# Gate layout with operands made another way, and 19 instead of 14 early first-layer products

## The chip, the cores and the metric

One core of a Trainium2 chip runs the whole program. The metric is the device time of one execution, in microseconds. Engines are named as in the profile: PE (matrix products; PEld is its weight load), DVE (vector), ACT (activation), POOL (GpSimd), SP (which here only issues DMAs).

## The reference, cut to what matters

One layer works on 1024 tokens of width 1024: a token mixer (gated linear attention and windowed attention), a layer norm, then a channel mixer that retrieves experts, and a last layer norm. The change lies in the channel mixer. For each token and each of 8 heads it takes the 16 best of 16384 experts by product keys (two lists of 128 keys); an expert has the number 128 * i1 + i2, a row u and a row v:

```
gate = jax.nn.softmax(top_s, axis=-1)
u = peer_u[eidx]
v = peer_v[eidx]
act = jax.nn.gelu(jnp.einsum('pd,phkd->phk', xt, u))
y = jnp.einsum('phk,phkd->pd', gate * act, v)
```

## The kernel before, in words

The kernel handles the channel mixer in two ways. For the first ND = 5 of 8 token tiles (640 tokens) it is **dense**: all 16384 experts are computed, as 128 expert tiles (jj) of 128 experts. A *product* (products(), L880 and below) is the first layer of one expert tile: the rows u are loaded in two pieces, split into a high part on ACT (uhi, L888) and a low part (ulo, L889), and two halves of 320 tokens are each summed from 8 x 3 matmuls (mm3, L115 to L117) into PSUM. Gelu, multiplication by the gates of that tile (L1059) and a split into high and low parts (L110, L111) give the weights W; outputs() then does the second layer for a pair of expert tiles (60 matmuls into pyd, added to yacc, L1087). For the last NS = 3 tiles (384 tokens) it is **sparse**: each step gathers the rows u, v of one expert for each of 128 tokens (L965) and uses DVE, ACT and POOL (L982, L998, L999).

**The gate layout** (gates(), L783 to L824) writes, for the 5 dense tiles, the gates as a dense array g_d of experts by tokens. It works on GG = 4 tokens at a time, 32 groups for each token tile, 160 in all. For each token, a matrix of 128 selected experts by 128 one-hot columns of i2 (oa) and one of i1 times the gate (ob), both in f32, are multiplied on PE (8 matmul instructions for a group, L819), and ACT copies the result out of PSUM (gstage, L821). Before, DVE makes both one-hots as wa and wb, bf16, with the four tokens innermost (L808, one instruction each); ACT copies wa into oa, with the tokens outermost (L809, one instruction); ob comes from wb in four ACT copies with the gate as scale (L815), in every fourth group instead in one DVE multiplication (L811). wa and wb share six buffers; oa and ob have four each.

**The order.** weave() (L95) takes generators, each with a number of steps and a span, and calls next() on them in the order of evenly spaced times. When it has used up all steps it runs each generator to its end, in the order in which they were given. After the token mixer one weave issues four: the gate layout (made, 152 steps), the retrieval for the last pair of token tiles (after = picks(3), 34 steps, span 0 to 0.7), the early products (early(), two steps for each) and the first 20 sparse steps. The retrieval of that pair has yielded once ahead of the weave (next(after), L869); it still has the 8 yields of best() and 13 in each of two calls of retrieval() (1 after the sums, 4 over the heads, 8 over the product sums, L733 to L740). What follows the last yield, such as chosen[j] at L760, runs when next() is called again. The order of issue is a priority only: a list scheduler puts each engine's instructions in an order of its own by estimated times, and each engine then runs in that order.

**Early products.** For the expert tiles in EARLY (0 to 3, then 12, 24, ... 120: 14) the product and its gelu are done in that weave, on the gate stage's PE, with the low part on POOL, and stored in act_d (L1014 to L1020). The loop of the dense stage (L1108 and below) loads them (gearly, L1054) and goes straight to the gates. The sparse steps are spread over the dense stage by progress (advance()).

In the profiled execution the token mixer takes the time up to about 860 us, the gate stage lasts from there to 1345, the dense stage from 1345 to the end.

Of the kernel before, what the change touches and what calls it, by code (L numbers as in the profile page):

```python
# [10 lines left out]
F32 = mybir.dt.float32  # L11
F32R = mybir.dt.float32r
BF = mybir.dt.bfloat16
I32 = mybir.dt.int32
U32 = mybir.dt.uint32
AF = mybir.ActivationFunctionType
OP = mybir.AluOpType
# [20 lines left out]
def kernel(ctx: ExitStack, tc: tile.TileContext, A, out):  # L38
    nc = tc.nc
    V, S, G, PE = nc.vector, nc.scalar, nc.gpsimd, nc.tensor  # L40

    def pool(stack, name, bufs=1, side="left", space=None):
        kw = {"space": space} if space == bass.MemoryType.DRAM else {"side": side, "reuse_waits": "tile"}
        if space == bass.MemoryType.PSUM:
            kw["space"] = space
        return stack.enter_context(tc.tile_pool(name=name, bufs=bufs, **kw))
# [6 lines left out]
    def acc(name):  # L53
        return ps.tile([128, 512], F32, tag="acc", name=name, bufs=4)
# [11 lines left out]
    iota = cst.tile([128, 128], F32, name="iota")  # L66
# [21 lines left out]
    g_d = drm.tile([TD // GT, 128, 128, GT], F32, name="g_d")  # L88
    act_d = [drm.tile([128, TD], F32, name=f"act_d{j}") for j in range(len(EARLY))]

# [4 lines left out]
    def weave(*parts):  # L95

        parts = [(g, n, *(at or (0, 1))) for g, n, *at in parts]
        order = sorted((a + (s + 0.5) / n * (b - a), i) for i, (_, n, a, b) in enumerate(parts) for s in range(n))
        for _, i in order:
            next(parts[i][0], None)  # L100
        for g, *_ in parts:
            for _ in g:
                pass
# [22 lines left out]
    with ExitStack() as px:  # L126
# [39 lines left out]
        early = px.enter_context(ExitStack())  # L166
# [278 lines left out]
    with ExitStack() as mx:  # L445
        xp = pool(mx, "xp", side="right")
        wb = pool(mx, "wb", side="right")
# [6 lines left out]
        def affine():  # L454
            pin(nc.scalar.dma_start(l1g, A["ln1_g"].to_broadcast([128, D])))
            pin(nc.scalar.dma_start(l1b, A["ln1_b"].to_broadcast([128, D])))
            pin(nc.scalar.dma_start(subk, A["subk"]))
            row = tk.tile([128, NCAND], F32, tag="c2", name="row", bufs=1)
            pin(nc.scalar.dma_start(row, A["iotac"].to_broadcast([128, NCAND])))
            V.tensor_copy(iotac, row[:, :, None].to_broadcast([128, NCAND, 8]))  # L460
            for i in range(2):
                nc.sync.dma_start(cols[:, i, :], mod_d[2 - i].rearrange("(k p) -> p k", p=128))
            V.tensor_scalar(cols[:, 0], cols[:, 0], 1.0, None, OP.add)
            yield
# [300 lines left out]
        def picks(pair, hh2):  # L765
            tv = tk.tile([128, 2, 2, NH, TOPK], F32, name="tv")
            ti = tk.tile([128, 2, 2, NH, TOPK], U32, name="ti")
            sc = []
            if pair == ORDER[-1]:
                for _ in scores(hh2, sc):  # L770
                    pass
            else:
                for a, b in zip(scores(hh2, sc), best(sc, tv, ti)):
                    yield
            yield
            if pair == ORDER[-1]:
                yield from best(sc, tv, ti)
            for i in range(2):
                yield from retrieval(2 * pair + i, tv[:, i], ti[:, i])

        gb, todo = [], []

        def gates():  # L783

            while not gb:
                yield
            wide = gb[0].tile([128, 128, GG], BF, name="wide", bufs=1)
            V.tensor_copy(wide, iota[:, :, None].to_broadcast([128, 128, GG]))
            for _ in range(ND):
                while not todo:  # L790
                    yield
                j = todo.pop(0)
                ej = gb[0].tile([128, 128], I32, name="ej", bufs=1)
                nc.sync.dma_start(ej, e_d[j])
                gj = gb[0].tile([128, 128], F32, name="gj", bufs=1)
                nc.sync.dma_start(gj, gt_d[j])
                i12 = gb[0].tile([128, 2, 128], I32, name="i12", bufs=1)
                V.tensor_scalar(i12[:, 0], ej, 127, None, OP.bitwise_and)
                V.tensor_scalar(i12[:, 1], ej, 7, None, OP.logical_shift_right)
                f12 = gb[0].tile([128, 2, 128], BF, name="f12", bufs=2)  # L800
                V.tensor_copy(f12, i12)
                for q in range(0, 128, GG):
                    if q % GT == 0:
                        gs = gb[0].tile([128, 128, GT], F32, name="gstage", bufs=2)
                    w = [gb[0].tile([128, 128, GG], BF, tag="wab", name=n, bufs=24 // GG) for n in ("wa", "wb")]
                    o = [gb[0].tile([128, GG, 128], F32, name=n, bufs=16 // GG) for n in ("oa", "ob")]
                    for i in range(2):
                        V.tensor_tensor(w[i], wide, f12[:, i, None, q:q + GG].to_broadcast([128, 128, GG]), OP.is_equal)  # L808
                    S.activation(o[0], w[0].rearrange("p i t -> p t i"), AF.Copy)  # L809
                    if SCALE[q // GG % len(SCALE)]:  # L810
                        V.tensor_tensor(o[1], w[1].rearrange("p i t -> p t i"),  # L811
                                        gj[:, q:q + GG, None].to_broadcast([128, GG, 128]), OP.mult)
                    else:
                        for c in range(GG):
                            S.activation(o[1][:, c], w[1][:, :, c], AF.Copy, scale=gj[:, q + c:q + c + 1])  # L815
                    for h in range(0, GG, 4):
                        p = acc("pgb")
                        for c in range(4):
                            PE.matmul(p[:, c::4], o[0][:, h + c], o[1][:, h + c], start=True, stop=True)  # L819
                        t = q % GT + h  # L820
                        S.activation(gs[:, :, t:t + 4], p.rearrange("p (j t) -> p j t", t=4), AF.Copy)  # L821
                    if q % GT == GT - GG:
                        nc.scalar.dma_start(g_d[128 // GT * j + q // GT], gs)
                    yield  # L824

        def pairs():
# [4 lines left out]
            while tiles or front or back or groups:  # L831
# [4 lines left out]
                for m in front + back:  # L836
                    m[1] += 1
                    try:
# [9 lines left out]
                        else:  # L848
                            back.remove(m)
                            if m[2] % 2:  # L850
                                yield m[2] // 2, hh2s[m[2] // 2]

        after, made = affine(), gates()
        turn = beat = 0.0
        for ready in pairs():
# [9 lines left out]
            if ready:  # L865
                for _ in after:
                    pass
                after = picks(*ready)
# [142 lines left out]
    with ExitStack() as gx:  # L1011
        ue = pool(gx, "ue", side="right")

        def early():  # L1014
            for i, jj in enumerate(EARLY):
                for h, p in products(jj, ue, ps, (3, 2, 2), G):
                    ga = ue.tile([128, HW], F32, name="gact", bufs=2)
                    S.activation(ga, p, AF.Gelu)
                    nc.sync.dma_start(act_d[i][:, HW * h:HW * h + HW], ga)
                    yield  # L1020

        steps = sparse_steps()

        def first():

            for _ in range(FIRST):
                next(steps)
                done[0] += 1
                yield

        done = [0]
        weave((made, GLEFT, *SPANS[0]), (after, 34, *SPANS[1]), (early(), 2 * len(EARLY), *SPANS[2]), (first(), FIRST, *SPANS[3]))
    px.close()
    front.close()

# [7 lines left out]
    def gated(jj, h):  # L1043
# [7 lines left out]
        w = wts[jj]  # L1051
        if jj in EARLY:
            ga = ep.tile([128, HW], F32, name="gearly", bufs=2)
            nc.sync.dma_start(ga, act_d[EARLY.index(jj)][:, HW * h:HW * h + HW])  # L1054
        else:
# [36 lines left out]
    yacc = ep.tile([128, ND, D], F32, name="yacc")  # L1092
    filled = [jj for jj in range(128) if jj not in EARLY][:FILL]
    for jj in filled:
# [36 lines left out]
WB = 7  # L1131
PICK = 1.3
GATE = 1
SCALE = (0, 0, 0, 1)
GLEFT = 152
SPANS = ((0, 1), (0, 0.7), (0.5, 1), (0.2, 0.8))
EARLY = [0, 1, 2, 3] + list(range(12, 128, 12))
UB = 3
BATCH = 2
FIRST = 20  # L1140
# [5 lines left out]
GG = 4  # L1146
# [118 lines left out]
```

## Time and profile before

| | us |
|---|---|
| median of 3 runs | 3193.69 |
| lowest, highest | 3190.36, 3199.3 |
| the profiled execution, its own time | 3201.31 |
| span of its profile | 3199.5 |

The span runs from the first to the last instruction; 1.8 us of the time lie around it. In a windows view each line gives a stretch, its length, the busy time of each engine (instructions counted as busy are joined where they overlap) with the number of instructions in brackets, the clock granted to PE as a share of full speed, the share of the DMA engines' time in use, and GB/s. In a groups view the number ahead of the bar is the count, behind it the busy time and the mean duration of one, then the idle time in front of such instructions and what ended it. Durations on one engine overlap a little, so the sum of busy times of groups can exceed the stretch.

### The profile page before, as it was taken

How to read it: one execution, taken by the hardware profiler on the slowest of the kernel's cores; microseconds unless marked ns; L12 is line 12 of the kernel's file. 1: busy time of each engine (PE TensorE's matmuls, PEld its weight loads, DVE VectorE, ACT ScalarE, POOL GpSimd, SP SyncE). 2: the span in 40 equal slices, each digit the busy share in tenths (PEclk: the TensorE clock that was granted, in tenths of full speed). 3: DMA queues.
4: the chain of work that ended last, by engine and by line, in shares of the span. 5: the costliest groups of instructions: out<-in, count | busy, mean ns of one | idle time of the engine just before them, and what ended most of it. 6: DMA issues, size and time to landing. Idle time of an engine off the chain costs nothing. (4 is left out here: it accounts for less than half of the span.)

```text
span 3199.5 us, 48912 instructions
## 1 busy us (share of the span) xinstructions
PE 2840.5 (89%) x16604; PEld 2456.4 (77%) x16604; DVE 2561.7 (80%) x5718; ACT 1614.6 (50%) x3437; POOL 1669.0 (52%) x1111
## 2 busy tenths in 40 slices
PE   6998878879777788789999999999999999999893
PEld 3677756757567787678889888888888888888782
DVE  4318834578788997469988988999988999999898
ACT  3324534342547889834555444555444545445452
POOL 0012301052543551026777776778768777778676
PEclk9999989889888899999999999999999999999996
DMA  9653655646465567577889898989889998989884
GB/s 331 218 188 112 215 213 198 213 171 207 148 219 186 227 217 265 221 235 284 321 323 327 314 328 305 321 322 336 328 310 326 331 328 304 323 307 330 295 292 171
DMA packets 352679, 848.82 MB, mean 265 GB/s; under 512 B 27627, under 2 KB 165611, under 8 KB 299692
## 3 DMA queue, kind: packets, MB, share of 16 engines
q1 hardware_dynamic: 285520, 384.20, 36.7%
q0 software_dynamic: 55296, 402.68, 33.0%
q10 hardware_dynamic: 11612, 58.81, 4.7%
q8 instruction: 131, 2.15, 0.3%
q14 instruction: 120, 0.98, 0.1%
HBM read 745.43 MB, written 100.16 MB: 264 GB/s over the span
## 5 line engine op out<-in xcount | busy, mean ns | idle before, releaser
L999 POOL TENSOR_TENSOR ys<-ys,uv 128x1024 f32<-128x1024 f32 x362 | 900.9, 2489 | 407.7 <-ACT uv L998 374.8
L117 PE MATMUL pact<-hhD,ulo 128*128 128x320 f32 x2048 | 633.4, 316 | 57.0 <-DVE ulo L889 36.7
L115 PE MATMUL pact<-hhD,uhi 128*128 128x320 f32 x2048 | 641.2, 314 | 5.8 <-ACT uhi L888 2.9
L116 PE MATMUL pact<-hhD,uhi 128*128 128x320 f32 x2048 | 638.0, 313 | 0.0
L115 PE MATMUL pyd<-vhi,W 128*128 128x512 f32 x1280 | 516.0, 403 | 39.8 <-DVE yacc L1087 32.9
L965 POOL DMA_INDIRECT uv<-in_uv_dram,ex x384 | 408.4, 1064 | 249.4 <-DVE ys L996 75.5
L116 PE MATMUL pyd<-vlo,W 128*128 128x512 f32 x1280 | 504.4, 394 | 0.0
L117 PE MATMUL pyd<-vhi,W 128*128 128x512 f32 x1280 | 502.6, 396 | 0.0
L998 ACT ACTIVATE uv<-uv,w 128x1024 f32<-128x1024 f32 x362 | 396.6, 1144 | 171.2 <-DVE w L987 105.2
L982 DVE SCALAR_TENSOR_TENSOR uv<-uv,h2p 128x1024 f32<-128x1024 f32 x384 | 462.8, 1208 | 11.6 <-DMA uv<-in_uv_dram,ex 7.5
L1087 DVE TENSOR_TENSOR yacc<-yacc,pyd 128x512 f32<-128x512 f32 x630 | 417.4, 676 | 45.3 <-PE pyd L117 43.2
L117 PEld LDWEIGHTS pact<-hhD,ulo 128*128 128x128 f32 x2048 | 388.9, 191 | 78.4 <-DVE ulo L889 47.0
L115 PEld LDWEIGHTS pact<-hhD,uhi 128*128 128x128 f32 x2048 | 392.7, 192 | 21.1 <-ACT uhi L888 4.5
L116 PEld LDWEIGHTS pact<-hhD,uhi 128*128 128x128 f32 x2048 | 392.1, 191 | 10.7
L115 PEld LDWEIGHTS pyd<-vhi,W 128*128 128x128 f32 x1280 | 243.0, 190 | 89.0 <-DVE yacc L1087 39.9
L889 DVE TENSOR_TENSOR ulo<-uraw,uhi 128x512 fp32r<-128x512 f32 x228 | 266.1, 1173 | 30.1 <-ACT uhi L888 28.2
L111 DVE TENSOR_TENSOR vlo<-vraw,vhi 128x512 fp32r<-128x512 f32 x256 | 279.3, 1112 | 10.4 <-ACT vhi L110 10.1
L117 PEld LDWEIGHTS pyd<-vhi,W 128*128 128x128 f32 x1280 | 242.2, 190 | 57.9
L116 PEld LDWEIGHTS pyd<-vlo,W 128*128 128x128 f32 x1280 | 243.6, 190 | 39.0
L819 PE MATMUL pgb<-ob,oa 128*128 128x128 f32 x1280 | 200.8, 306 | 54.7 <-ACT ob L815 42.5
L819 PEld LDWEIGHTS pgb<-ob,oa 128*128 128x128 f32 x1280 | 182.5, 208 | 69.7 <-ACT ob L815 53.1
L110 ACT ACTIVATE W<-pact 128x320 fp32r<-128x320 f32 x222 | 95.5, 431 | 240.8 <-DVE pact L1059 234.6
(357 smaller groups left out, 5234.1 us busy)
## 6 DMA issues: line engine op xcount, KB each, us to landing
uraw<-in_ut_dram SPq DMA_DIRECT2D x256, 256.0 KB
vraw<-in_uv_dram SPq DMA_DIRECT2D x256, 256.0 KB
g_d<-gstage ACTq DMA_DIRECT2D x20, 2048.0 KB
gload<-g_d SPq DMA_DIRECT2D x32, 1280.0 KB
wo<-wo_d SPq DMA_DIRECT2D x64, 512.0 KB
wq<-wq_d SPq DMA_DIRECT2D x64, 512.0 KB
wt<-in_w_ada_dram SPq DMA_DIRECT2D x48, 512.0 KB
wq_d<-wqs SPq DMA_DIRECT2D x16, 512.0 KB
```

Source lines behind the costliest of these rows:

```text
L110: S.activation(hi, src, AF.Copy)
L111: eng.tensor_tensor(lo, src, hi.bitcast(F32), OP.subtract)
L115: PE.matmul(out_, l[0], r[0], start=(k == 0), stop=False)
L116: PE.matmul(out_, l[0], r[1], start=False, stop=False)
L117: PE.matmul(out_, l[1], r[0], start=False, stop=(k == n - 1))
L819: PE.matmul(p[:, c::4], o[0][:, h + c], o[1][:, h + c], start=True, stop=True)
L889: lower.tensor_tensor(lo, raw, hi.bitcast(F32), OP.subtract)
L965: G.indirect_dma_start(out=uv[n][0].rearrange("p a d -> p (a d)"), out_offset=None, in_=A["uv"], in_offset=bass.IndirectOffsetOnAxis(ap=ch ...
L982: pin(V.scalar_tensor_tensor(t[:, 0], t[:, 0], 1.0, h2[j], OP.mult, OP.mult, accum_out=w[:, i:i + 1]))
L998: S.activation(v, v, AF.Copy, scale=wb)
L999: G.tensor_tensor(ys[j], ys[j], v, OP.add)
L1087: V.tensor_tensor(ya, ya, p, OP.add)
```

## The change

The gate layout gets a second flag list, `retrieved`, and two branches. Without the flag, DVE writes oa itself, as f32 (comparing a plain row of numbers with each token's i2), makes wb as before, and all four scaled copies into ob are ACT's, in every group. With the flag, wa goes through ACT as before, and ob comes from four DVE instructions on 128 x 128, each a comparison and a multiplication by the gate. The flag is set by rest(), a generator that runs the retrieval of the last pair to its end and then appends to the list; it takes the place of `after` in the weave, with the same 34 steps. A bf16 copy of the row (once) and an f32 copy of i1 (f2, once for each token tile) are added. SCALE is gone. The span of the retrieval goes from 0.7 to 0.6 and that of the early products begins at 0.35 instead of 0.5. EARLY becomes 0 to 3 and 8, 16, ... 120: 19 expert tiles.

```
--- before.py
+++ after.py
@@ -778,7 +778,7 @@
             for i in range(2):
                 yield from retrieval(2 * pair + i, tv[:, i], ti[:, i])
 
-        gb, todo = [], []
+        gb, todo, retrieved = [], [], []
 
         def gates():
 
@@ -786,6 +786,8 @@
                 yield
             wide = gb[0].tile([128, 128, GG], BF, name="wide", bufs=1)
             V.tensor_copy(wide, iota[:, :, None].to_broadcast([128, 128, GG]))
+            row = gb[0].tile([128, 128], BF, name="iotab", bufs=1)
+            V.tensor_copy(row, iota)
             for _ in range(ND):
                 while not todo:
                     yield
@@ -799,20 +801,31 @@
                 V.tensor_scalar(i12[:, 1], ej, 7, None, OP.logical_shift_right)
                 f12 = gb[0].tile([128, 2, 128], BF, name="f12", bufs=2)
                 V.tensor_copy(f12, i12)
+                f2 = gb[0].tile([128, 128], F32, name="f2", bufs=2)
+                V.tensor_copy(f2, i12[:, 1])
+
+                def wide_hot(i, q):
+
+                    w = gb[0].tile([128, 128, GG], BF, tag="wab", name=("wa", "wb")[i], bufs=24 // GG)
+                    V.tensor_tensor(w, wide, f12[:, i, None, q:q + GG].to_broadcast([128, 128, GG]), OP.is_equal)
+                    return w
+
                 for q in range(0, 128, GG):
                     if q % GT == 0:
                         gs = gb[0].tile([128, 128, GT], F32, name="gstage", bufs=2)
-                    w = [gb[0].tile([128, 128, GG], BF, tag="wab", name=n, bufs=24 // GG) for n in ("wa", "wb")]
                     o = [gb[0].tile([128, GG, 128], F32, name=n, bufs=16 // GG) for n in ("oa", "ob")]
-                    for i in range(2):
-                        V.tensor_tensor(w[i], wide, f12[:, i, None, q:q + GG].to_broadcast([128, 128, GG]), OP.is_equal)
-                    S.activation(o[0], w[0].rearrange("p i t -> p t i"), AF.Copy)
-                    if SCALE[q // GG % len(SCALE)]:
-                        V.tensor_tensor(o[1], w[1].rearrange("p i t -> p t i"),
-                                        gj[:, q:q + GG, None].to_broadcast([128, GG, 128]), OP.mult)
+                    if retrieved:
+                        w = wide_hot(0, q)
+                        S.activation(o[0], w.rearrange("p i t -> p t i"), AF.Copy)
+                        for c in range(GG):
+                            V.tensor_scalar(o[1][:, c], iota, f2[:, q + c:q + c + 1], gj[:, q + c:q + c + 1],
+                                            OP.is_equal, OP.mult)
                     else:
+                        V.tensor_tensor(o[0], row[:, None, :].to_broadcast([128, GG, 128]),
+                                        f12[:, 0, q:q + GG, None].to_broadcast([128, GG, 128]), OP.is_equal)
+                        w = wide_hot(1, q)
                         for c in range(GG):
-                            S.activation(o[1][:, c], w[1][:, :, c], AF.Copy, scale=gj[:, q + c:q + c + 1])
+                            S.activation(o[1][:, c], w[:, :, c], AF.Copy, scale=gj[:, q + c:q + c + 1])
                     for h in range(0, GG, 4):
                         p = acc("pgb")
                         for c in range(4):
@@ -1029,7 +1042,12 @@
                 yield
 
         done = [0]
-        weave((made, GLEFT, *SPANS[0]), (after, 34, *SPANS[1]), (early(), 2 * len(EARLY), *SPANS[2]), (first(), FIRST, *SPANS[3]))
+        def rest():
+
+            yield from after
+            retrieved.append(True)
+
+        weave((made, GLEFT, *SPANS[0]), (rest(), 34, *SPANS[1]), (early(), 2 * len(EARLY), *SPANS[2]), (first(), FIRST, *SPANS[3]))
     px.close()
     front.close()
 
@@ -1131,10 +1149,9 @@
 WB = 7
 PICK = 1.3
 GATE = 1
-SCALE = (0, 0, 0, 1)
 GLEFT = 152
-SPANS = ((0, 1), (0, 0.7), (0.5, 1), (0.2, 0.8))
-EARLY = [0, 1, 2, 3] + list(range(12, 128, 12))
+SPANS = ((0, 1), (0, 0.6), (0.35, 1), (0.2, 0.8))
+EARLY = [0, 1, 2, 3] + list(range(8, 128, 8))
 UB = 3
 BATCH = 2
 FIRST = 20
```

## Rows read from the trace of the kernel before

**Rows 1.** The page: busy shares, then PE over 40 equal slices.

```profile
PE 2840.5 (89%) x16604; PEld 2456.4 (77%) x16604; DVE 2561.7 (80%) x5718; ACT 1614.6 (50%) x3437; POOL 1669.0 (52%) x1111
PE   6998878879777788789999999999999999999893
```

**Rows 2.** Windows of the gate stage: columns as named in its first line.

```profile
core 0: us, PE busy (x) PEld busy (x) DVE busy (x) ACT busy (x) POOL busy (x), PEclk, DMA share, GB/s
1100.00:1183.00 83.00, 66.51 (x453) 65.27 (x452) 80.64 (x175) 64.25 (x159) 45.31 (x41) 0.89 0.57 208
1183.00:1226.00 43.00, 42.96 (x325) 42.77 (x324) 33.04 (x64) 41.44 (x109) 14.61 (x12) 1.00 0.77 289
1226.00:1345.00 119.00, 87.32 (x506) 75.95 (x504) 71.27 (x155) 118.58 (x311) 7.88 (x9) 0.93 0.56 214
860.00:1345.00 485.00, 383.23 (x2544) 355.84 (x2544) 396.52 (x1405) 380.62 (x964) 169.21 (x177) 0.90 0.62 221
```

**Rows 3.** Two lines of the kernel: last product sums and early gelus, first and last start.

```profile
L740 DVE TENSOR_REDUCE ee<-oh x64: 388/833/1734, 674.7 to 1180.0; 128x16 f32<-128x160 f32 x24, 128x16 f32<-128x400 f32 x24, 128x16 f32<-128x320 f32 x8, 128x16 f32<-128x800 f32 x8
...
L1018 ACT ACTIVATE gact<-pact x28: 409/418/469, 1020.0 to 1225.3; 128x320 f32<-128x320 f32 x28
```

**Rows 4.** Groups by line, 1226 to 1345: xcount | busy us, mean ns | idle, releaser.

```profile
L815 ACT ACTIVATE ob<-wb,gj 128x128 f32<-128x128 bf16 x180 | 60.3, 415 | 0.0
L809 ACT ACTIVATE oa<-wa 128x512 f32<-128x512 bf16 x60 | 40.2, 674 | 0.0
L821 ACT ACTIVATE gstage<-pgb 128x512 f32<-128x512 f32 x64 | 37.6, 599 | 0.5 <-PE pgb L819 0.5
L808 DVE TENSOR_TENSOR wa<-wide,f 128x512 bf16<-128x512 bf16 x57 | 24.1, 422 | 21.6 <-ACT ob L815 13.1 <-ACT oa L809 7.5 <-ACT gstage L821 0.8
L811 DVE TENSOR_TENSOR ob<-wb,gj 128x512 f32<-128x512 bf16 x15 | 10.4, 691 | 1.4
```

**Rows 5.** Groups by line, 1100 to 1183: the operands on DVE.

```profile
L808 DVE TENSOR_TENSOR wa<-wide,f 128x512 bf16<-128x512 bf16 x28 | 16.8, 599 | 0.0
L811 DVE TENSOR_TENSOR ob<-wb,gj 128x512 f32<-128x512 bf16 x7 | 6.2, 888 | 0.1
```

**Rows 6.** Groups by line, 855 to 1345: the ACT parts of a product.

```profile
L888 ACT ACTIVATE uhi<-uraw 128x512 fp32r<-128x512 f32 x28 | 17.2, 624 | 2.6 <-issue 1.8 <-POOL ce L709 0.8
L1018 ACT ACTIVATE gact<-pact 128x320 f32<-128x320 f32 x28 | 11.8, 424 | 0.9 <-PE pact L117 0.8
```

**Rows 7.** Groups by line, 1183 to 1226: one gstage copy for each group.

```profile
L821 ACT ACTIVATE gstage<-pgb 128x512 f32<-128x512 f32 x17 | 9.9, 581 | 0.8 <-PE pgb L819 0.8
```

**Rows 8.** Windows 1698.6 to 3050.8: eight stretches of six pairs, one and sum.

```profile
2038.00:2201.20 163.20, 161.28 (x890) 144.81 (x889) 151.37 (x243) 85.62 (x146) 130.08 (x72) 1.00 0.92 331
...
sum 1352.20, PE 1305.54 PEld 1165.83 DVE 1239.30 ACT 675.30 POOL 1003.49; mean PE 163.19 PEld 145.73 DVE 154.91 ACT 84.41 POOL 125.44
```

**Rows 9.** Windows of two pairs: with one product, with two.

```profile
2038.00:2058.90 20.90, 20.90 (x110) 18.29 (x109) 18.50 (x28) 11.48 (x18) 17.56 (x10) 1.00 0.89 326
2058.90:2086.90 28.00, 28.00 (x158) 25.34 (x157) 25.48 (x44) 14.81 (x26) 24.44 (x14) 1.00 0.99 357
```

**Rows 10.** Windows of the eight pairs ahead of those of rows 11: sum.

```profile
sum 250.50, PE 233.02 PEld 208.82 DVE 227.42 ACT 119.16 POOL 183.50; mean PE 29.13 PEld 26.10 DVE 28.43 ACT 14.89 POOL 22.94
```

**Rows 11.** Windows of the eight pairs that begin those stretches (early tile): sum.

```profile
sum 173.40, PE 173.40 PEld 152.35 DVE 160.33 ACT 87.53 POOL 124.67; mean PE 21.68 PEld 19.04 DVE 20.04 ACT 10.94 POOL 15.58
```

**Rows 12.** Groups by line, 1500 to 2900: products and gating on DVE.

```profile
L889 DVE TENSOR_TENSOR ulo<-uraw,uhi 128x512 fp32r<-128x512 f32 x182 | 212.3, 1173 | 10.4 <-ACT uhi L888 8.8 <-ACT uv L998 0.7 <-issue 0.2
L1059 DVE TENSOR_TENSOR pact<-pact,gload 128x320 f32<-128x320 f32 x182 | 89.0, 489 | 31.6 <-ACT pact L1057 29.5 <-ACT uv L998 1.6 <-issue 0.3
L111 DVE TENSOR_TENSOR W<-pact,W 128x320 fp32r<-128x320 f32 x182 | 87.4, 481 | 16.1 <-ACT W L110 11.5 <-ACT uv L998 4.4
L111 DVE TENSOR_TENSOR W<-gearly,W 128x320 fp32r<-128x320 f32 x18 | 24.3, 1368 | 0.5 <-ACT W L110 0.5
L1059 DVE TENSOR_TENSOR gearly<-gearly,gload 128x320 f32<-128x320 f32 x16 | 10.8, 715 | 4.3 <-DMA gload<-g_d 4.1
```

## The prediction

> **What bounds the kernel now.** The page comes first: PE is busy for 89% of the span, and its slices read 7 and 8 up to about the fifteenth and 9 from the twentieth on [rows 1]. So there are two regimes, a gate stage in which PE has room and a dense stage in which it has hardly any. The change moves five products from the second to the first.
>
> The windows show what bounds the gate stage [rows 2]. From 1100 to 1183, while the last retrieval runs (its last sums start at 1180, [rows 3]), DVE is busy for 80.6 of 83 us. From 1183 to 1226 both ACT (41.4) and PE (43.0) fill the 43 us, with the last products in them (the last gelu starts at 1225, [rows 3]). From 1226 to 1345 only gate groups and a few sparse steps are left, ACT is busy for 118.6 of 119 us and PE for 87.3. So DVE bounds until 1183, ACT after that. Of the 160 groups, each with one gstage copy, 17 + 64 = 81 come after 1183 [rows 4, 7] and 79 before.
>
> In the dense stage a pair of expert tiles is the unit, counted from its first matmul into pyd to the next pair's. A pair with two products takes 28.0 us with PE busy for all of them, one with a single product (the other tile is early) 20.9 [rows 9]. A product is therefore worth **7.1 us** where PE bounds. Eight stretches of six pairs, one of the six early in each, take 1352.2 us, 169.0 each [rows 8], against 5 x 28.0 + 20.9 = 160.9 with PE full: 8.1 us are lost elsewhere. DVE is busy for 1239 of the 1352 us, so it stands close behind PE.
>
> **First, what the change does.** The second way of making the operands is never used. rest() has 34 steps in the weave, and the retrieval has 34 yields left: 8 from best(), 13 from each of two tiles. The 34th step stops at the last yield. The flag is set behind it, at a 35th call, and that comes only when weave() runs its generators out; the gate layout stands first there and has used up its 160 groups by then. So all 160 groups take the branch without the flag: oa from DVE in f32, all of ob on ACT, no 128x128 DVE comparisons.
>
> **Gate stage, DVE.** A group loses wa and a fourth of an ob multiplication and gains one f32 comparison of 128x512. No row shows that comparison. Below, it costs what wa does (599 ns while POOL works, 422 later), above, what L811 does, 888 and 691 ns [rows 4, 5]. I take the upper end: L811 has the same shape, f32 output and one operand spread over the innermost axis. Each of the 79 groups before 1183 costs 888 - 599 - 7/28 x 888 = 67 ns more: **+5 us** on the engine that bounds there; at the lower end 222 ns less, -18. The f2 and row copies are six small instructions, under 599 ns each: +1, at most 4. wb stays, and neither removed instruction has anyone else waiting on it.
> VectorE: DVE Perf Modes in the Trainium skill (section "Mode 2×_1P — pack two bf16 into one 32-bit read") says that two results a cycle need every tensor to be 16-bit. That speaks against the change: the f32 output would take the slow rate, which is the upper end; if the fast rate held, the sum would be 23 us lower.
>
> **Gate stage, ACT.** In the last window ACT's groups add up to 138 us in 118.6 busy ones [rows 2, 4], so instructions overlap and each counts 0.85 of its duration. A group loses oa (0.85 x 674 = 573 ns) and gains a fourth of four ob copies (353 ns): -220 ns; -18 us for the 81 groups after 1183. An added product brings two uhi and two gelus, 0.85 x 2 x (624 + 424) ns [rows 6] = 1.8 us: +9 for five. Net **-9 us** where ACT bounds.
>
> **Gate stage, PE.** The five products bring 5 x 7.1 = 36 us. PE idles for 102 of 485 us there, 32 of them after 1226 [rows 2]. If all five come after 1226, PE needs 87.3 + 36 = 123 us for what took 119: +4. If some find room before, as the earlier span allows, ACT sets the end: -9. I take about 0 (-9 to +4), nearer PE's end, since PE was full whenever products ran after 1183. The low parts are POOL's, which is busy for 7.9 us after 1226. The ten added loads from SP's queue and ten stores of gelus fall where DMA is at 0.56 to 0.77. SP waits for nothing new. The earlier retrieval span shifts DVE work ahead of gate groups without adding any; nothing. Gate stage: +5 + 1 + 0 = **+6 us**, the end moving from 1345 to 1351.
>
> **Dense stage.** Five tiles lose their products, so early pairs come every fourth instead of every sixth. With PE full, the 60 pairs from expert tile 8 on take 15 x (3 x 28.0 + 20.9) = 1574 instead of 10 x 160.9 = 1609: **-36 us**. What becomes of the other loss, 8.1 us in six pairs, decides the rest. The pair ahead of an early one takes 250.5 / 8 = 31.3 us [rows 10], the early one 173.4 / 8 = 21.7 [rows 11], the other 32 of the 48 take (1352.2 - 250.5 - 173.4) / 32 = 29.0 [rows 8]. An early tile thus saves 29.0 - 21.7 = 7.3 and costs its forerunner 2.3: 5.0 each, **-25 us** for five. The ends: if the loss is spread by time, 36 x 169.0 / 160.9 = -37; if it all hangs on early tiles, 15 x 8.1 - 10 x 8.1 = 40 us come back, +5. I keep the measured split.
> DVE gains nothing from an early tile: it saves two ulo (1173 ns each), but both halves of its gating read SBUF instead of PSUM, 715 against 489 and 1368 against 481 ns [rows 12], which is 2.2 us given back of 2.3. SBUF — State Buffer in the Trainium skill (section "SBUF: two separate sides") says that a DVE instruction with two SBUF inputs and a GpSimd one that reads SBUF exclude each other for a whole instruction; the 1368 agrees. The sparse steps are spread over 117 units of progress instead of 119.5, so they keep their pace in time, and DMA at about 0.9 stays there: the rows u of five tiles go, the stored gelus come.
>
> **Sum.** +6 - 25 = **-19 us**. The profiled execution took 3201.3 us (span 3199.5 and 1.8 around it), 7.6 above the median 3193.7; I apply the difference to the median: **3175 us**. A change under 0.3%, 9.6 us, can hardly be told from none; faster means under 3184, slower over 3203.
>
> **Rivals.**
> The dense stage gives its full PE share (-37) and ACT sets the end of the gate stage without DVE being later (-9): 3194 - 46 = 3148; a comparison at wa's price takes off 18 more at the utmost. For it: pairs run at exactly 28.0 at a time. Against it: DVE close behind PE. Chance 0.15, faster.
> DVE takes PE's place: early tiles carry most or all of the loss, the dense stage comes out between -6 and +5, and with the gate stage's +6 the time is 3194 to 3205. For it: DVE at 1239 of 1352 us with its work unchanged. Against it: the measured 2.3 is not 8.1. Chance 0.2, mostly no change.
> Slower: PE's fixed order puts the five products between the last gate groups, and ACT waits at gstage behind them. Then the 36 us come on top of the last stretch, whose 32 us of PE idle time stay: +36 + 6 - 25 = +17, **3211 us**. It decides if the idle time after 1226 is not filled by more than 8 us. For it: between 1183 and 1226 PE is already full. Against it: three buffers of raw rows and POOL at 7.9 of 119 us let products run ahead. Chance 0.13.
> The flag does come in time: ACT's part of a late group falls to oa and gstage, 0.85 x (674 + 599) = 1.1 us, PE's +4 sets the end after 1226, 3175 to 3179. Chance 0.02; it would show in DVE instructions of 128x128 in gates().
>
> **How the numbers follow.** The forecast has 0.5. Faster: 0.45 of it (its own range is 3160 to 3187), 0.15 of the first rival and the flag's 0.02: 0.62. No change: 0.05 of the forecast and 0.18 of the second rival: 0.23. Slower: the third rival and 0.02 of the second: 0.15. The range goes from 3148, the first rival without its utmost, to 3203, the second rival's end; it leaves out the slow case and a few hundredths below.
>
> **What would show it.** After the change there must be 160 DVE comparisons into oa of 128x512 f32 near 690 to 890 ns, 640 ACT copies into ob, none into oa. The gate stage should end within 8 us of 1351, with ACT below 119 of its last 119 us and PE above 100. In the dense stage 15 pairs of about 21 us, forerunners near 31. I am wrong if the comparison takes 420 ns, if the gate stage ends over 15 us off, or if the pairs without an early neighbour grow beyond 29.5, with DVE as what PE waits for.

## The result, and the profile after

The kernel after takes **3232.15 us** (median of 4 runs, 3226.78 to 3236.67), that before 3196.49 beside it; the ratio is 1.0114, interval 1.0095 to 1.0132. It is slower by some 36 us, where 3175 was forecast. The profiled execution has a span of 3228.4 us, 28.9 more than before.

The page of the kernel after, as in [rows 1]:

```profile
PE 2840.1 (88%) x16604; PEld 2456.1 (76%) x16604; DVE 2638.9 (82%) x5674; ACT 1573.1 (49%) x3437; POOL 1689.9 (52%) x1121
PE   6998878978778889898999899999999999999980
```

DVE is busy for 77 us more, PE for as long as before. Windows show where. First the kernel before: the gate stage stands in [rows 2]; here are the 63 pairs, from the first matmul into pyd to that of the last pair, and the rest.

```profile
1370.70:3131.40 1760.70, 1690.20 (x9110) 1504.83 (x9109) 1598.95 (x2520) 868.36 (x1497) 1274.48 (x718) 0.99 0.87 313
3131.40:3199.50 68.10, 17.15 (x62) 12.49 (x60) 56.01 (x70) 18.75 (x26) 41.60 (x20) 0.63 0.42 162
```

The kernel after: the gate stage, the 63 pairs, the rest (columns as in [rows 2]).

```profile
860.00:1326.00 466.00, 392.90 (x2771) 373.73 (x2770) 423.38 (x1355) 345.16 (x968) 188.57 (x187) 0.94 0.66 236
1351.60:3121.60 1770.00, 1675.92 (x8870) 1483.28 (x8869) 1621.12 (x2482) 843.47 (x1459) 1237.11 (x696) 0.97 0.85 304
3121.60:3228.40 106.80, 17.77 (x62) 12.87 (x60) 79.55 (x98) 32.68 (x43) 79.65 (x42) 0.59 0.54 211
```

The first pair starts at 1351.6 instead of 1370.7, **19 us earlier**. The pairs take **9 us longer**, with 240 matmuls less. From the last pair's start to the end it takes **39 us longer**. -19 + 9 + 39 = 29, the whole difference.

Of these 19 us, 7 lie ahead of the change. The token mixer, the same code in both kernels, ends with this instruction on DVE (eight of them, duration min/median/max in ns, first and last start); the last one starts at 852.9 before and at 845.9 after:

```profile
L111 DVE TENSOR_TENSOR mT<-ao,mT x8: 661/678/693, 458.8 to 852.9; 128x512 fp32r<-128x512 f32 x8
L111 DVE TENSOR_TENSOR mT<-ao,mT x8: 667/678/692, 454.5 to 845.9; 128x512 fp32r<-128x512 f32 x8
```

From there to the end of the last gstage copy (1344.8 and 1325.9) the gate stage takes 492 us before and 480 after: it is **12 us shorter**. The change costs 36 us by the traces, then, as it does by the medians.

**The gate stage.** Groups by line, 860 to 1326, of the kernel after:

```profile
L828 ACT ACTIVATE ob<-wb,gj 128x128 f32<-128x128 bf16 x624 | 205.0, 411 | 3.5 <-DMA gj<-gt_d 2.9 <-DVE wb L810 0.6
L824 DVE TENSOR_TENSOR oa<-iotab,f 128x512 f32<-128x512 bf16 x156 | 125.2, 809 | 15.9 <-PE pgb L832 15.4
L834 ACT ACTIVATE gstage<-pgb 128x512 f32<-128x512 f32 x160 | 94.1, 595 | 31.9 <-PE pgb L832 24.9 <-DMA hhD<-hh_d 6.5 <-ACT ob L828 0.2
```

There are no 128x128 comparisons on DVE and no ACT copies into oa: the flag comes too late. The comparison takes 809 ns in the mean, between 691 and 888 [rows 4, 5]. ACT is busy for 345 instead of 381 us, PE for 393 of the 466 us, DVE for 423.

**The end.** The sparse steps' products (L982 before, L995 after; two instructions a step) from the last pair's start on, in windows of that line alone. Before:

```profile
3131.40:3199.50 68.10, 0.00 (x0) 0.63 0.42 162
```

After:

```profile
3121.60:3228.40 106.80, 14.52 (x24) 0.59 0.54 211
```

Before, no sparse step is left when the last pair starts; after, **twelve** are. The timeline of the kernel after shows what this does (lines left out):

```profile
3180.85 2.33 POOL L1012 TENSOR_TENSOR ys<-ys,uv 128x1024 f32<-128x1024 f32 x1
...
3183.21 0.32 SPq L1020 DMA_DIRECT2D y_d<-ys  x1
...
3185.87 0.32 SPq L944 DMA_DIRECT2D late<-y_d  x1
...
3189.37 1.50 DVE L949 TENSOR_TENSOR late<-late,rows 128x1024 f32<-128x1024 f32 x1 [2.57 <-DMA late<-y_d]
```

The last sparse sum is stored at 3183, loaded again and normalised from 3189 on, and the norms of the dense tiles stand behind it on DVE. Before, the last step's product is done ahead of the last pair, and these norms run beside that pair.

**The pairs.** Groups by line in the dense stage of the kernel before, from its first pair to the end:

```profile
L987 DVE TENSOR_TENSOR w<-w,gate 128x2 f32<-128x2 f32 x182 | 63.9, 352 | 4.7 <-ACT w L986 4.7
L111 DVE TENSOR_TENSOR W<-gearly,W 128x320 fp32r<-128x320 f32 x26 | 30.2, 1182 | 0.6 <-ACT W L110 0.5
L1059 DVE TENSOR_TENSOR gearly<-gearly,gload 128x320 f32<-128x320 f32 x26 | 15.3, 627 | 21.0 <-DMA gload<-g_d 19.3 <-DMA gearly<-act_d 1.5
```

The same three of the kernel after:

```profile
L1000 DVE TENSOR_TENSOR w<-w,gate 128x2 f32<-128x2 f32 x182 | 85.3, 468 | 5.1 <-ACT w L999 5.1
L111 DVE TENSOR_TENSOR W<-gearly,W 128x320 fp32r<-128x320 f32 x36 | 48.4, 1360 | 0.1
L1077 DVE TENSOR_TENSOR gearly<-gearly,gload 128x320 f32<-128x320 f32 x36 | 34.8, 1003 | 25.5 <-DMA gload<-g_d 25.0 <-DMA gearly<-act_d 0.5
```

All three have both inputs in SBUF, and together they take 59 us more; the last two also serve five more tiles. Instructions that read PSUM keep their price (489 and 481 ns, as in [rows 12]). The longer ones meet POOL: of the 38 W instructions of early tiles after (two halves for each of 19), 7 overlap no POOL instruction in the trace and take 487 ns in the mean, the other 31 take 1501; of those with an input in PSUM none takes more than 494.

What PE waited for in the pairs, before and then after (total us, times, longest):

```profile
PE pact L117 <- DVE ulo L889: 35.0, 28, 4.2
PE pyd L115 <- DVE yacc L1087: 27.7, 15, 6.1
```

```profile
PE pact L117 <- DVE ulo L902: 47.3, 33, 4.1
PE pyd L115 <- DVE yacc L1105: 38.2, 24, 7.5
```

PE is idle for 71 of the 1761 us before and for 94 of the 1770 after; DVE ended 63 and 86 of them.

### The profile page after: what moved, and what is told of

It is laid out like the page before. It is cut to its first block, busy times and chain, and to the rows that moved or that the text cites. A ratio compares the mean times of both kernels' runs of the same rounds, so it can differ in the third digit from the quotient of the medians.

```text
span 3228.4 us, 48977 instructions
## 1 busy us (share of the span) xinstructions
PE 2840.1 (88%) x16604; PEld 2456.1 (76%) x16604; DVE 2638.9 (82%) x5674; ACT 1573.1 (49%) x3437; POOL 1689.9 (52%) x1121
## 5 line engine op out<-in xcount | busy, mean ns | idle before, releaser
L117 PE MATMUL pact<-hhD,ulo 128*128 128x320 f32 x2048 | 642.5, 319 | 66.4 <-DVE ulo L902 47.8
L115 PE MATMUL pact<-hhD,uhi 128*128 128x320 f32 x2048 | 649.1, 318 | 6.0 <-ACT uhi L901 5.2
L116 PE MATMUL pact<-hhD,uhi 128*128 128x320 f32 x2048 | 644.4, 316 | 0.0
L995 DVE SCALAR_TENSOR_TENSOR uv<-uv,h2p 128x1024 f32<-128x1024 f32 x384 | 462.7, 1209 | 13.9 <-DMA uv<-in_uv_dram,ex 13.7
L115 PEld LDWEIGHTS pact<-hhD,uhi 128*128 128x128 f32 x2048 | 397.0, 194 | 22.1 <-ACT uhi L901 8.5
L116 PEld LDWEIGHTS pact<-hhD,uhi 128*128 128x128 f32 x2048 | 396.7, 194 | 10.4
L111 DVE TENSOR_TENSOR vlo<-vraw,vhi 128x512 fp32r<-128x512 f32 x256 | 294.6, 1172 | 9.6 <-ACT vhi L110 9.4
L902 DVE TENSOR_TENSOR ulo<-uraw,uhi 128x512 fp32r<-128x512 f32 x218 | 245.2, 1129 | 34.1 <-ACT uhi L901 32.5
L832 PE MATMUL pgb<-ob,oa 128*128 128x128 f32 x1280 | 184.6, 287 | 36.5 <-ACT ob L828 18.2
L828 ACT ACTIVATE ob<-wb,gj 128x128 f32<-128x128 bf16 x640 | 209.9, 411 | 10.9 <-DVE wb L810 8.0
```

What stands on the lines that cost most here:

```text
L111: eng.tensor_tensor(lo, src, hi.bitcast(F32), OP.subtract)
L115: PE.matmul(out_, l[0], r[0], start=(k == 0), stop=False)
L116: PE.matmul(out_, l[0], r[1], start=False, stop=False)
L117: PE.matmul(out_, l[1], r[0], start=False, stop=(k == n - 1))
L828: S.activation(o[1][:, c], w[:, :, c], AF.Copy, scale=gj[:, q + c:q + c + 1])
L902: lower.tensor_tensor(lo, raw, hi.bitcast(F32), OP.subtract)
```

## The experiments

Theories are numbered as they came up. The table has the median, the ratio to the kernel before run beside it, and from each trace the start of the first pair, the length of the 63 pairs, the time from the last pair's start to the end, and the sparse steps left at that start. The token mixer, which no run changes, ends up to 12 us earlier than in the trace of before (845.9 after, 851.3 in e1, 843.6 in e2, 844.6 in e15), so "first pair" compares two traces no better than that.

| run | us | ratio [interval] | first pair | 63 pairs | to the end | left |
|---|---|---|---|---|---|---|
| before | 3196 | 1 | 1371 | 1761 | 68 | 0 |
| after | 3232 | 1.0114 [1.0095, 1.0132] | 1352 | 1770 | 107 | 12 |
| e1 operands only | 3170 | 0.9930 [0.9908, 0.9953] | 1356 | 1746 | 68 | 0 |
| e2 early tiles and spans only | 3245 | 1.0166 [1.0132, 1.0201] | 1376 | 1759 | 109 | 12 |
| e3 flag in time | 3226 | 1.0119 [1.0084, 1.0153] | 1355 | 1757 | 109 | 12 |
| e4 SHARE 0.94 | 3213 | 1.0058 [1.0033, 1.0083] | 1354 | 1763 | 101 | 10 |
| e5 after, PSUM copy | 3164 | 0.9909 [0.9880, 0.9939] | 1354 | 1710 | 105 | 12 |
| e6 before, PSUM copy | 3185 | 0.9979 [0.9961, 0.9996] | 1364 | 1752 | 65 | 0 |
| e7 before, less PE | 3219 | 1.0087 [1.0057, 1.0116] | 1366 | 1742 | 108 | 12 |
| e8 before, more DVE | 3225 | 1.0106 [1.0077, 1.0136] | 1372 | 1787 | 65 | 0 |
| e9 after, 32 steps ahead | 3200 | 1.0024 [0.9999, 1.0049] | 1367 | 1765 | 66 | 0 |
| e10 e1 and PSUM copy | 3168 | 0.9931 [0.9907, 0.9954] | 1342 | 1758 | 66 | 0 |
| e11 e5 and 32 steps | 3165 | 0.9927 [0.9905, 0.9949] | 1361 | 1731 | 63 | 0 |
| e12 before, 8 steps ahead | 3208 | 1.0063 [1.0040, 1.0087] | 1358 | 1739 | 108 | 12 |
| e13 after, early tiles shifted | 3195 | 0.9995 [0.9977, 1.0013] | 1357 | 1738 | 100 | 11 |
| e14 e5 and 26 steps | **3145** | 0.9841 [0.9808, 0.9873] | 1363 | 1703 | 85 | 5 |
| e15 operands and spans | 3177 | 0.9944 [0.9928, 0.9960] | 1337 | 1763 | 69 | 0 |
| e16 e13 and e14 | 3148 | 0.9859 [0.9839, 0.9880] | 1356 | 1712 | 81 | 5 |

**The two halves of the change.** e1 is the kernel after with EARLY and SPANS of before, e2 the kernel before with those of after:

```
-SPANS = ((0, 1), (0, 0.6), (0.35, 1), (0.2, 0.8))
-EARLY = [0, 1, 2, 3] + list(range(8, 128, 8))
+SPANS = ((0, 1), (0, 0.7), (0.5, 1), (0.2, 0.8))
+EARLY = [0, 1, 2, 3] + list(range(12, 128, 12))
```

> The kernel after, with the 14 early tiles and the spans of before: only the operands are made another way. Theory 1 (DVE bounds the dense stage, and early tiles add DVE time there): the dense stage is that of before, so the time is that of before less what the gate stage saves, 5 to 20 us, some 3175 to 3190. Theory 2 (any change of the program makes the list scheduler order the dense stage anew, and that order costs the 49 us): the dense stage is longer than before here too, by 20 us or more, though nothing in it has changed.

> The kernel before, with the 19 early tiles and the spans of after, the operands made as before. Theory 1: the dense stage lengthens as in the kernel after, by 35 to 60 us, and DVE is busy some 45 us more in it; the gate stage, bound by ACT, takes 5 to 20 us more than before: slower than the kernel after, about 3235 to 3265. Theory 2: the dense stage lands anywhere within 25 us of before.

The operands alone **gain 0.7%**, the early tiles alone **lose 1.7%**. The last gstage copy ends at 1344.8 before, 1325.4 in e1, 1325.9 after and 1346.8 in e2. Counted from the end of the token mixer the gate stage takes 492 us before, 474 in e1, 480 after and 503 in e2: the operands save 18 us, the five added products cost 6 to 11, with their spans. Four traces of the same gate layout (after, e4, e5, e13) give 476 to 484, so 4 us either way are no difference. e1 came out 5 us below theory 1's range and e2 within it, but not by theory 1's way: in e2 the pairs are as long as before, and its longer dense stage is the end alone, 40 us. Of these two runs only the one with the 19 early tiles has a longer dense stage.

**The flag, and the pace.** e3 gives the retrieval its 35th step, e4 changes one constant (the weave line is cut).

```
-        weave((made, GLEFT, *SPANS[0]), (rest(), 34, *SPANS[1]), ...
+        weave((made, GLEFT, *SPANS[0]), (rest(), 35, *SPANS[1]), ...
-SHARE = 0.98
+SHARE = 0.94
```

> The kernel after with 35 steps instead of 34 for the retrieval, so that the flag is set inside the weave and some 60 late groups take the second way (wa through ACT, ob by four DVE instructions). The gate stage: ACT has 1.1 us instead of 1.7 us a late group, PE and DVE set its end; within 10 us of the kernel after either way. By theory 1 the dense stage keeps its length within 10 us of the kernel after; by theory 2 it moves by more.

> The kernel after with SHARE 0.94 instead of 0.98, so that the sparse steps are spread over 4 per cent less progress. Theory 3 (the end is late only because the sparse steps are paced too slowly against PE, as the 39 us more behind the last pair's start suggest): the end falls by 20 to 35 us, to about 3200, and the pairs stay as they are. Theory 1: the DVE time is the same, so what the end gains the pairs lose: within 12 us of 3232.

With the flag in time 244 DVE comparisons of 128x128 appear (413 ns each), and the gate stage ends at 1326.7 instead of 1325.9, 6 us longer from the end of the token mixer: the second way is worth nothing here. e4 came down by some 19 us against the kernel after and fits neither theory: ten sparse steps are left instead of twelve, and the end is only 6 us shorter. So how far behind PE the program issues them explains little of it.

**PE and DVE by themselves.** e5 (on after) and e6 (on before) let ACT copy the stored gelu into PSUM (indices of act_d cut):

```
-            ga = ep.tile([128, HW], F32, name="gearly", bufs=2)
-            nc.sync.dma_start(ga, act_d[...][...])
+            raw = ep.tile([128, HW], F32, name="gearly", bufs=2)
+            nc.sync.dma_start(raw, act_d[...][...])
+            ga = pe.tile([128, 512], F32, tag="trp", name="gacc", bufs=3)[:, :HW]
+            S.activation(ga, raw, AF.Copy)
```

> The kernel after, with the stored gelu of an early tile copied by ACT into a PSUM buffer, so that the gating of early tiles reads PSUM on DVE like that of the others (38 halves). Theory 1 (DVE's busy time bounds the dense stage, and an early tile costs it because its gating has two inputs in SBUF and waits for POOL): DVE loses 38 x ((976 - 489) + (1314 - 481)) ns = 50 us in the dense stage, and the dense stage shortens by 35 to 50 us, to a time of about 3185. Theory 4 (the sparse steps have a pace of their own of some 4.8 us, and with less PE work they simply end behind it): DVE loses as much, but the last sparse step stays within 10 us and the time within 12 us of 3230.

> The kernel before, with the same copy into PSUM for its 14 early tiles. Theory 1: DVE loses 28 x ((617 - 489) + (1132 - 481)) ns = 22 us, the time falls by 12 to 22 us, to about 3177. Theory 4: within 8 us of before.

e5 gains more than theory 1 forecast, 68 us by the medians, and e6 less, 8 us; over the span DVE is busy 54 us less in e5 and 3 us less in e6.

e7 leaves a third of the matmuls of 15 products out (the other tiles keep mm3), e8 adds a DVE instruction to each pair (lines cut in both):

```
+                if jj in range(9, 128, 8):
+                    PE.matmul(p[:, :HW], l[0], r[0], start=(k == 0), stop=False)
+                    PE.matmul(p[:, :HW], l[1], r[0], start=False, stop=(k == KC - 1))
```

```
+                if (t, n) == (2, 0):
+                    V.tensor_reduce(junk, p, AX.X, OP.max)
```

> The kernel before, with one of the three matmuls left out in the products of 15 expert tiles (9, 17, ... 121): 240 matmuls, the PE work of five products, and nothing else. It leaves the high weight part times low token part out of these products. If PE bounds the dense stage, as predicted: 25 to 36 us less, about 3163. Theory 1 and theory 4: within 10 us of before, since neither DVE nor the sparse steps have less to do.

> The kernel before, with one more DVE instruction for each pair of expert tiles, a maximum over 512 columns of PSUM that nothing uses, some 0.65 us, 42 us in all. Theory 1: the dense stage lengthens by 25 to 42 us, to about 3230. If PE bounds: under 12 us. Theory 4: under 12 us as long as the sparse steps keep their pace.

e7 is the telling one: less work for PE and nothing else makes the kernel **slower by 0.9%**, which no theory had. The windows of e7, pairs and rest:

```profile
1365.90:3107.60 1741.70, 1659.85 (x8870) 1465.64 (x8870) 1593.59 (x2492) 851.52 (x1478) 1238.68 (x697) 0.99 0.86 309
3107.60:3216.00 108.40, 19.97 (x62) 13.44 (x60) 78.21 (x98) 33.64 (x45) 80.08 (x41) 0.58 0.54 209
```

The end is the kernel after's, 40 us longer, with twelve sparse steps left. The later end thus needs no added early tile. The pairs are 19 us shorter, but they have lost 36 us of PE work (5 x 7.1) and those twelve steps too, so this is no price of PE work alone. e8's group in the dense stage:

```profile
L1085 DVE TENSOR_REDUCE junk<-pyd 128x1 f32<-128x512 f32 x64 | 43.5, 680 | 5.4 <-PE pyd L117 5.2
```

These 43.5 us lengthen the pairs by 26 and the dense stage by 22, near theory 1's 25 to 42; but differences of about 20 us also come without a cause that these runs show (e12 and e15, below). With the waits of PE above: PE is busy for most of the pairs, and when it is idle it mostly waits for DVE. In e5 the pairs fall by 60 us and the end stays at 105 with its twelve steps: the two losses are separate. A group of the kernel after, then three of e5, dense stage:

```profile
L111 DVE TENSOR_TENSOR vlo<-vraw,vhi 128x512 fp32r<-128x512 f32 x253 | 292.7, 1178 | 9.6 <-ACT vhi L110 9.4
```

```profile
L111 DVE TENSOR_TENSOR vlo<-vraw,vhi 128x512 fp32r<-128x512 f32 x255 | 318.8, 1270 | 27.5 <-ACT vhi L110 27.5
L1079 DVE TENSOR_TENSOR gacc<-gacc,gload 128x320 f32<-128x320 f32 x37 | 18.1, 491 | 3.0 <-ACT gacc L1074 2.3 <-issue 0.4
L111 DVE TENSOR_TENSOR W<-gacc,W 128x320 fp32r<-128x320 f32 x38 | 17.8, 483 | 1.1 <-ACT W L110 1.0
```

The gating costs 491 and 483 ns again, and some of what it saves comes back at vlo, 1270 ns instead of 1178.

**The balance of sparse steps.** e9 puts 32 instead of 20 of them into the gate stage of the kernel after (FIRST = 32), e12 only 8 into that of before, with PE's work as it was.

> The kernel after with 32 instead of 20 sparse steps in the gate stage. Theory 5 (two separate losses: DVE's gating of early tiles makes the pairs longer, and the work taken from PE lets the list scheduler run PE ahead of the sparse steps, 12 of which are left at the last pair's start, which makes the end 39 us later): no or few sparse steps are left at the last pair's start, the stretch from there to the end falls from 107 to some 68 us, the pairs stay within 12 us of the kernel after's 1770, and the gate stage takes 12 x 2.8 = 34 us more of DVE time, of which 10 to 30 show: 3205 to 3225. Theory 1 alone (only DVE's busy time counts): the steps moved are the same DVE time, so the end stays within 10 us of 3230.

> The kernel before with 8 instead of 20 sparse steps in the gate stage, nothing taken from PE. Theory 5: the same end as in the kernel after without its early tiles, some 12 steps left at the last pair's start and 95 to 110 us from there to the end instead of 68; the gate stage, bound by ACT at its end, saves 0 to 15: 3205 to 3235. Theory 1 alone: 12 x 2.8 us of DVE time move from one stage to the other, no more than 10 us either way.

What theory 5 says of the end came out in both; the time of e9, 3200, lies 5 us below its range. Windows of the rest, in e9 and then in e12:

```profile
3131.90:3197.80 65.90, 16.92 (x62) 11.92 (x60) 57.06 (x68) 19.30 (x27) 39.21 (x19) 0.66 0.40 158
```

```profile
3097.40:3205.20 107.80, 17.31 (x62) 11.37 (x60) 76.90 (x100) 33.71 (x45) 81.11 (x43) 0.61 0.54 210
```

Twelve steps fewer ahead and the later end appears in a kernel that has none of the change; twelve more and it is gone, for a first pair 16 us later. What decides is the number of sparse steps against PE work in the dense stage. Windows of the 63 pairs with the sparse products alone, DVE's busy time and in brackets the instructions, two a step: before, after, e4 and e12.

```profile
1370.70:3131.40 1760.70, 441.60 (x728) 0.99 0.87 313
1351.60:3121.60 1770.00, 426.90 (x704) 0.97 0.85 304
1354.30:3116.90 1762.60, 428.95 (x708) 0.98 0.86 306
1358.30:3097.40 1739.10, 441.66 (x728) 0.99 0.89 318
```

The pairs hold 364 steps where they have some 9110 matmuls and 352 to 354 where they have 8870. In all eighteen traces that is one step for 25.0 to 25.2 matmuls, whatever pace the program asks for (e4) and however many steps lie ahead (e9, e12). So the list scheduler's order lets the steps go by PE work and not by the program's progress: with 240 matmuls less, ten to twelve steps find no place. Why its estimates give a step 25 matmuls was not tried. e12 shows one thing more: its pairs have the matmuls and the steps of those before, and are 22 us shorter.

**Versions with both mended.** e10 is e1 with the PSUM copy, e11 and e14 are e5 with FIRST = 32 and 26.

> The operands of the kernel after, the 14 early tiles and spans of before, and the stored gelu copied into PSUM by ACT. If the two gains are independent of each other: the 24 us of the operands and the 8 us that the copy gave before add up, 3155 to 3168. If the list scheduler's order decides, it lands outside of that.

> The kernel after with the copy into PSUM and with 32 sparse steps in the gate stage. Theory 5: the pairs keep the 60 us that the copy gave, and the stretch from the last pair's start falls from 105 to some 68; with 10 to 30 us more in the gate stage 3135 to 3160, the fastest so far. Theory 1 alone: within 10 us of 3164.

> The kernel after with the copy into PSUM and with 26 sparse steps in the gate stage, halfway between 20 (3164) and 32 (3165). Theory 5: some 6 sparse steps left at the last pair's start, an end between 63 and 105 us behind it, a gate stage of 4 to 8 us less than with 32: 3150 to 3168.

e14 is the fastest, **0.984 of the kernel before**, 5 us faster than its forecast; e11 missed its range by 5 us, since its pairs are 21 us longer than e5's while its end fell as forecast. In e10, at the upper end of its range, the copy added next to nothing: with 14 early tiles DVE's busy time in the pairs is 1600 us as in e1.

**What is left of the pairs.** In e13 the later early tiles are at 10, 18, ... 122 (range(10, 128, 8)), in e16 too, with the edits of e14; e15 is e1 with the spans of after.

> The kernel after with the 15 later early tiles at 10, 18, ... 122 instead of 8, 16, ... 120, so that an early tile is the third and not the first of the four tiles that one load of gates (gload, 1.25 MB) serves. Theory 6 (the pairs are longer because DVE, in order, stands up to 10 us at the gating of an early tile until that load has landed, 25 us in all, and PE then waits for yacc): these waits vanish and the pairs shorten by 15 to 30 us, from 1770 to about 1748, while the end behind the last pair stays near 107: about 3208. Theory 1 (the two SBUF inputs alone): the pairs stay within 8 us of 1770, about 3230.

> Both at once: the early tiles at 10, 18, ... 122, the copy into PSUM, and 26 sparse steps in the gate stage. If the shift of 32 us in the pairs and the 60 us of the copy take away the same DVE time at the early tiles' gating, the pairs stay within 12 us of the 1703 that the copy reached without the shift: 3135 to 3157. If they are two separate losses, the pairs fall by some 30 more, to about 1673, near what PE needs: 3110 to 3125.

> The operands and the spans of the kernel after with the 14 early tiles of before: against the run with the gates alone (3170) only the order of issue in the gate stage differs. If the spans do nothing, as predicted: within 8 us of 3170, the dense stage within 8 us too. Theory 2 (any new order moves the dense stage by tens of us): outside of that.

e13's pairs are 32 us shorter and its time 37, but not for theory 6's reason: DVE's waits for the gate load stay, 23.5 us against 25.0. Waits and groups of e13:

```profile
DVE gearly L1077 <- DMA gload<-g_d: 23.5, 5, 10.1
```

```profile
L111 DVE TENSOR_TENSOR W<-gearly,W 128x320 fp32r<-128x320 f32 x36 | 32.3, 909 | 0.8 <-ACT W L110 0.7
```

W falls from 1360 to 909 ns: 22 of the 38 meet a POOL instruction instead of 31, so the place of an early tile decides how often its gating meets POOL. With the copy the shift brings nothing more (e16, pairs 1712 against 1703), as if both took away the same loss.

e15 differs from e1 in the order of the gate stage alone. Its time is within the forecast, its dense stage is not: it is 17 us longer, all of it in the pairs. With the 22 us of e12, differences of some 20 us in the pairs may be nothing but order, or one execution against another: the 9 us between before and after are among them, and the 24 between e1 and after are hardly more. The 60 us of e5 are beyond it. e15 is also the nearest partner of the kernel after, which differs from it in EARLY alone: the five products cost 11 us of gate stage (469 to 480 from the end of the token mixer), 7 us of pairs and 38 us at the end.

## Why the prediction was wrong

- **The flag** is never set in time, as predicted, and the comparison has a price near the upper end, 809 ns. Right.
- **The gate stage** was forecast 6 us longer and is 12 us shorter. The step that failed is "Gate stage, PE", with its "about 0 (-9 to +4), nearer PE's end". It lets the five products eat up all of the 18 us that ACT saves; they cost 6 to 11 us, so that ACT's end of that range, -9, is the nearer one. The DVE term of +6 does not show either: the operands alone were worth -18 + 5 + 1 = -12 by these steps, and e1 measured -18, which is ACT's term by itself. That a group which DVE delays is only made later on would explain it and was not tried.
- **The pairs** were forecast 25 us shorter and are 9 longer, with twelve sparse steps less in them. The step that failed is "An early tile thus saves 7.3 and costs its forerunner 2.3", with the rest of the pairs held at 29.0. From the fifth pair to the 62nd, cut at each pair's first matmul into pyd, the forerunners take 31.4 us (31.3 in the forecast), but the early pairs 23.2 instead of 21.7 and all others 29.5 instead of 29.0: 22 and 14 us. It priced the gating at 715 and 1368 ns; over the same stretch, 1500 to 2900, it came to 1262 and 1531. w<-w,gate, which the forecast left out, rose from 352 to 468 ns over the dense stage. e5 shows the size: without two SBUF inputs at the gating the pairs take 60 us less. How much of the 34 us that the forecast missed is order is open. The second rival, DVE in PE's place, is nearest to what the pairs do.
- **The end** is the term that was missing, 39 us, and alone larger than the error allowed. The sentence that failed is that the sparse steps "keep their pace in time": they keep it against PE's matmuls, 25 to a step, so that with 240 matmuls less twelve were left over. e7 shows it without the change, e12 with fewer steps ahead, and e9 takes it away with more.
- The slower rival had the sign right and the mechanism wrong: the gate groups were not delayed.

Against before, the operands alone gain 25 us (e1), with the new spans 20 (e15). The early tiles lose 50 with the operands of before and the new spans (e2), and 55 with the new operands (after against e15). e1 and e2 add up to 25 us where the whole change costs 36: some 10 us are order, or the two halves are not independent.

## What to carry to other kernels

Before work is taken from the engine that is full, look for the stream that was balanced against it: where two streams end together, a shorter one only makes the other the end, and what stood behind the last of them comes later with it. Test that with an edit that removes the work and nothing else, as e7 does, before the real change is priced. And where a second engine is busy for nearly as long (here DVE, 1599 us of the pairs' 1761), price what a change does to that engine's instructions, above all those that read two inputs from SBUF while POOL works.

## What was not expected of the hardware

A DVE instruction on 128x2 elements (w<-w,gate) took 352 ns in the mean before and 468 after, for the same work. Where no POOL instruction overlaps it, it takes 147 and 148 ns; where one does, 527 before and 810 after. The time that DVE lost at one instruction with two SBUF inputs seems to move in part to others of its kind when the first is given a PSUM input: vlo rose from 1178 to 1270 ns in e5, though w<-w,gate fell to 297. So such losses are to be counted over all instructions with two SBUF inputs together, not line by line.
